# Which queue loads the weights of a scan's columns: SyncE's or GpSimd's

## The chip, the cores and the metric

The kernel runs on one core of one Trainium2 chip. The metric is the device time of one execution in microseconds. The engines are called as in the profile: PE (TensorE's matmuls), PEld (its weight loads), DVE (VectorE), ACT (ScalarE), POOL (GpSimd) and SP (SyncE, which here only issues DMAs). A DMA can be issued by SP or by POOL; each issues in the order of its own program, and a DMA that has to wait keeps all that stands behind it on that engine waiting.

## The reference

A trunk of two layers is applied to two groups of 512 tokens (s = 0 and 1) with 1024 channels, with the same weights. The first layer is a time mixing with a scan in both directions:

```
xn = rms_norm(x); lerp(j) = xn + (0.5*(x_prev + x_next) - xn) * mu[j]
r, k, v, z = lerp(0) @ w_r, lerp(1) @ w_k, lerp(2) @ w_v, xn @ w_z
for d in (forward, backward):
    decay, a = f(lerp(3+d)), g(lerp(5+d))          # two low-rank products each
    S_t = S_{t-1} (diag(decay_t) + a_t b_t^T) + v_t k_t^T ;  y_t = S_t r_t
x1 = x + rms_norm((norm(y_fwd + y_bwd) + bonus) * silu(z) @ w_o)
```

The second layer is attention in a neighbourhood of an 8 x 64 grid, with a gate:

```
q, k, v, z = split(rms_norm(x1) @ w_in + b_in)
out = x1 + rms_norm((attention(q, k, v, rpb) * silu(z)) @ w_ao + b_o)
```

All is float32.

## The kernel before

**Products with weights.** A weight matrix is cut into columns of 128 outputs. One column is a tile of 128 x 1024 (512 KB), loaded in two halves of 128 x 512 (256 KB) into the tile `raw`, which has three buffers (NRAW). Each half is split into a high and a low part (`whi`, a cast on ACT; `wlo`, a subtraction on DVE), and PE does three matmuls for each of the eight blocks of 128 inputs. Such a block of three matmuls is called a product below. A `raw` buffer is free again when the subtraction has read it. `whi` and `wlo` have four buffers each.

**Stages.** The prelude (to about 155 us) normalizes, makes the inputs and computes the first columns of s = 0. Then comes the scan (`scan_phase`, 155 to 1155 us): 8 blocks (two groups of tokens, four blocks of heads), each with 8 steps, one after the other. A step is a short chain through PE, ACT and DVE (`step`, `factors`, `near`, `outer`), and each block needs a preparation (`prep`: the decays, the tile `ab`, stored as `dab`) and an inverse of triangular matrices (`inverse`: the tile `MT`). Between these, PE computes 80 columns of weights, which are 160 halves: r and v of s = 0, k, r, v and z of s = 1, w_o, and 24 columns of w_in. The rest (`rest`, attention and the last products) follows to the end. It loads its weights with `self.load`, on SP.

**The columns in the scan** are `flow`. Its parts are generators: `loads` (line 719 issues a load), `splits` (line 726 the cast on ACT, line 728 the subtraction on DVE), `operands` (lines 752 and 754 split the inputs), `products` (lines 807 to 809) and `posts` (what is done with a column's result).

**The order.** A planner (`Clock` and `weave`) sets the order of PE, DVE and ACT in the scan. It keeps a rough time for each engine and lets that generator go on which can go on first. A DMA of SP's counts 380 ns of issue time in it, one of POOL's 900. Where nothing is ready for PE for some time, it puts in a fill matmul of 128x256 (line 1631), whose result nobody reads. The order of SP and POOL is then made by the framework's scheduler.

**Who issues what in the scan.** SP issues the weight loads, the loads of each step (`cab` from `dab`, `V` and `X` from `dvt`), those of each preparation (`k`, `r`, `rb`, `tmp` from the low-rank weights), the stores of `dab`, and the loads of the columns' inputs (`xr`). POOL issues the stores of the columns' results (`dr`, `dv`, `dk`, `dz`, `dq`, line 327; `dvt`, line 690) and of `dks`, and it fills small tiles: a column of `e` at each preparation (line 898) and half of `MT` at each inverse (line 1019, a pair of fills). Before the first block it fills the two `MT` tiles (line 1662). What goes to which queue is set here:

```
    def store(self, kind):
        return self.nc.gpsimd if self.away and kind not in ("y", "x1", "h") else self.nc.sync

    def load(self, dst, src):
        self.nc.sync.dma_start(dst, src)
        return dst
```

`away` is true in the scan alone.

Of the kernel before, what the change touches and what calls it, by code (L numbers as in the profile page):

```python
# [19 lines left out]
P = 128  # L20
# [211 lines left out]
class Trunk:  # L232
# [470 lines left out]
    def flow(self):  # L703


        nc, did, ck = self.nc, self.did, self.clock
# [3 lines left out]
        raw, w, x, todo = {}, {}, {}, {}  # L710
# [4 lines left out]
        def loads():  # L715
            for c, (_, _, src, _) in enumerate(cols):
                for j in range(2):
                    yield "S", lambda: did["load"] < did["split"] + self.NRAW
                    raw[2 * c + j] = self.load(self.t("raw", (P, self.WP), self.NRAW), src[:, j * self.WP:(j + 1) * self.WP])
                    did["load"] += 1  # L720

        def splits():
# [92 lines left out]
        def posts(a):  # L815
# [5 lines left out]
        few = lambda: did["split"] - did["k"] // 4 <= self.STOCK  # L821
        return [
            Thread(lambda: 0, loads()), Thread(lambda: 3 if few() else 9, splits()), Thread(lambda: 0, fetched()), Thread(lambda: 2.5, operands()),
            Thread(lambda: 0.6, residual()), Thread(lambda: 0.6, scaled()), Thread(lambda: 0.6, squares()),
            Thread(lambda: 9, products()), Thread(lambda: 2, posts(0)), Thread(lambda: 2, posts(1))]
# [1097 lines left out]
```

## Time and profile before

| | |
|---|---|
| time, median of 3 runs | 1673.4 us (1672.16 to 1676.07) |
| the profiled execution | 1673.62 us, span 1671.8 us |
| granted TensorE clock, mean | 0.974 |
| busy: PE, DVE, ACT, POOL | 1566.5, 1229.4, 982.8, 116.9 us |
| SP's hardware queue | 194144 packets, 301.84 MB |
| POOL's software queue | 10112 packets, 31.47 MB |

Shares and sums of the whole span mix the stages. The change lies in the scan, so its part is read by stretches. A row "A L1 <- B L2: t, n, m" in the view of waits says that engine A stood idle t us in all, n times, at most m us, ahead of an instruction of line 1, and that line 2 on engine B ended the wait. SPq is SP's queue of DMA issues.

### The profile page before, as it was taken

How to read it: one execution, taken by the hardware profiler on the slowest of the kernel's cores; microseconds unless marked ns; L12 is line 12 of the kernel's file. 1: busy time of each engine (PE TensorE's matmuls, PEld its weight loads, DVE VectorE, ACT ScalarE, POOL GpSimd, SP SyncE). 2: the span in 40 equal slices, each digit the busy share in tenths (PEclk: the TensorE clock that was granted, in tenths of full speed). 3: DMA queues.
4: the chain of work that ended last, by engine and by line, in shares of the span. 5: the costliest groups of instructions: out<-in, count | busy, mean ns of one | idle time of the engine just before them, and what ended most of it. 6: DMA issues, size and time to landing. Idle time of an engine off the chain costs nothing.

```text
span 1671.8 us, 46461 instructions
## 1 busy us (share of the span) xinstructions
PE 1566.5 (94%) x18834; PEld 1200.3 (72%) x18834; DVE 1229.4 (74%) x2725; ACT 982.8 (59%) x1977; POOL 116.9 (7%) x246
## 2 busy tenths in 40 slices
PE   7989897999999988999998999999999898999998
PEld 6867666776767766766776777777778687777776
DVE  8985667788877885897888897855676856554564
ACT  5443665766766667655675665454577655554562
POOL 0000102310101122000000000000000000000000
PEclk9989998999999997999998999999999999999999
DMA  6435678677687786776776665563774337545553
GB/s 210 164 126 187 200 259 270 199 240 225 214 258 239 220 268 184 232 249 198 239 235 217 204 225 189 169 193 128 269 239 150 116 114 263 178 158 176 160 175 107
DMA packets 204470, 336.27 MB, mean 201 GB/s; under 512 B 20928, under 2 KB 86592, under 8 KB 204256
## 3 DMA queue, kind: packets, MB, share of 16 engines
q1 hardware_dynamic: 194144, 301.84, 56.4%
q0 software_dynamic: 10112, 31.47, 5.7%
q8 instruction: 148, 2.42, 0.6%
q14 instruction: 66, 0.54, 0.1%
HBM read 227.71 MB, written 105.51 MB: 199 GB/s over the span
## 4 chain that ended last, share of the span: by engine, by line
PE 68%; DVE 12%; DMA 9%; ACT 7%; issue 4%; SPq 1%; DVEq 0%; ACTq 0%
PE pm L807 7%; PE pm L808 5%; PE pm L809 5%; PE pg L428 5%; PE pg L429 5%; PE pg L430 5%; PE pf L1095 3%; PE zy L1167 2%; PE us L1214 2%; PE sc L1442 2%; PE us L1194 2%; PE zy L1218 2%; PE po L1475 2%; PE pt L1460 2%; DMA dab<-ab 1%
## 5 line engine op out<-in xcount | busy, mean ns | idle before, releaser
L807 PE MATMUL pm<-act,whi 128*128 128x512 f32 x640 | 285.5, 446 | 12.7 <-ACT act L776 4.1
L808 PE MATMUL pm<-act,whi 128*128 128x512 f32 x640 | 256.5, 401 | 9.8 <-DVE act L754 5.9
L809 PE MATMUL pm<-act,wlo 128*128 128x512 f32 x640 | 255.7, 400 | 7.9 <-DVE wlo L728 7.8
L428 PE MATMUL pg<-act,whi 128*128 128x512 f32 x448 | 182.6, 409 | 6.1 <-ACT act L377 5.7
L429 PE MATMUL pg<-act,whi 128*128 128x512 f32 x448 | 178.0, 397 | 0.1
L430 PE MATMUL pg<-act,wlo 128*128 128x512 f32 x448 | 177.0, 395 | 0.0
L377 ACT CAST whi<-raw 128x512 fp32r<-128x512 f32 x148 | 91.5, 619 | 125.2 <-PE pg L429 80.7
L807 PEld LDWEIGHTS pm<-act,whi 128*128 128x128 f32 x640 | 122.0, 191 | 56.2 <-issue 11.6
L809 PEld LDWEIGHTS pm<-act,wlo 128*128 128x128 f32 x640 | 122.3, 191 | 38.9 <-DVE wlo L728 12.1
L378 DVE TENSOR_TENSOR wlo<-raw,whi 128x512 fp32r<-128x512 f32 x148 | 101.3, 687 | 66.0 <-ACT whi L377 58.8
L808 PEld LDWEIGHTS pm<-act,whi 128*128 128x128 f32 x640 | 122.8, 192 | 35.8 <-DVE act L754 11.1
L728 DVE TENSOR_TENSOR wlo<-raw,whi 128x512 fp32r<-128x512 f32 x160 | 108.9, 685 | 41.4 <-ACT whi L726 41.2
L726 ACT CAST whi<-raw 128x512 fp32r<-128x512 f32 x160 | 97.9, 618 | 55.4 <-PE pm L808 38.5
L428 PEld LDWEIGHTS pg<-act,whi 128*128 128x128 f32 x448 | 84.6, 189 | 24.8 <-ACT act L377 6.0
L430 PEld LDWEIGHTS pg<-act,wlo 128*128 128x128 f32 x448 | 84.8, 189 | 18.7 <-issue 1.2
L429 PEld LDWEIGHTS pg<-act,whi 128*128 128x128 f32 x448 | 84.9, 190 | 17.2 <-issue 1.7
L999 DVE TENSOR_TENSOR etmp<-N 128x30 f32<-128x30 f32 (+14 forms) x240 | 78.5, 327 | 4.1
L1001 DVE TENSOR_TENSOR N<-etmp,N 128x30 f32<-128x30 f32 (+14 forms) x240 | 78.5, 327 | 3.8
L1453 DVE CUSTOM_DVE_ANT_0 sb<-sc,bias 128x256 f32<-128x256 f32 x128 | 49.4, 419 | 28.9 <-PE pt L1460 22.9
L1456 ACT ACTIVATE sb<-sb,mx 128x256 f32<-128x256 f32 x128 | 64.0, 505 | 8.7 <-DVE mx L1455 8.6
L1206 ACT COPY X<-us 64x256 f32<-64x256 f32 x128 | 46.8, 366 | 35.6 <-PE zy L1073 32.9
L1095 PE MATMUL pf<-cab 64*64 64x128 f32 (+1 forms) x2048 | 66.3, 266 | 0.7 <-issue 0.7
(396 smaller groups left out, 3465.3 us busy)
## 6 DMA issues: line engine op xcount, KB each, us to landing
dab<-ab SPq DMA_DIRECT2D x32, 1024.0 KB
cab<-dab SPq DMA_DIRECT2D x64, 512.0 KB
raw<-in_w_in_dram SPq DMA_DIRECT2D x128, 256.0 KB
bias<-in_rpb_dram SPq DMA_DIRECT2D x32, 384.0 KB
raw<-in_w_z_dram SPq DMA_DIRECT2D x32, 256.0 KB
raw<-in_w_k_dram SPq DMA_DIRECT2D x32, 256.0 KB
raw<-in_w_r_dram SPq DMA_DIRECT2D x32, 256.0 KB
k<-dk SPq DMA_DIRECT2D x32, 256.0 KB
```

Of the source, the lines that this page charges most:

```text
L377: self.nc.scalar.copy(hi, src)
L378: (eng or self.nc.vector).tensor_tensor(lo, src, hi.bitcast(F32), op=ALU.subtract)
L428: nc.tensor.matmul(ps, hi, x[k][0], start=(k == 0), stop=False)
L429: nc.tensor.matmul(ps, hi, x[k][1], start=False, stop=False)
L430: nc.tensor.matmul(ps, lo, x[k][0], start=False, stop=(k == KT - 1))
L726: nc.scalar.copy(hi, raw[h])
L728: nc.vector.tensor_tensor(lo, raw.pop(h), hi.bitcast(F32), op=ALU.subtract)
L807: nc.tensor.matmul(ps, hi[:, at], xh, start=(k == 0), stop=False)
L808: nc.tensor.matmul(ps, hi[:, at], xl, start=False, stop=False)
L809: nc.tensor.matmul(ps, lo[:, at], xh, start=False, stop=(k == KT - 1))
L999: vt.tensor_tensor(tv, N[:, q + 1:, q:q + 1].broadcast_to([P, n, q]), N[:, q:q + 1, :q].broadcast_to([P, n, q]), op=ALU.mult)
L1095: end = nc.tensor.matmul(st.f[half(a), h, 0, d, g] if st.last else st.f[half(a), h, :, d, g], ab[half(h), d, g, 2 * e[d] + 1 - a], rt if s ...
```

## The change

In `loads`, the weight halves are issued with `nc.gpsimd.dma_start` in place of `self.load`. That is all; lines below 719 get a number that is one higher.

```
--- before.py
+++ after.py
@@ -716,7 +716,8 @@
             for c, (_, _, src, _) in enumerate(cols):
                 for j in range(2):
                     yield "S", lambda: did["load"] < did["split"] + self.NRAW
-                    raw[2 * c + j] = self.load(self.t("raw", (P, self.WP), self.NRAW), src[:, j * self.WP:(j + 1) * self.WP])
+                    raw[2 * c + j] = self.t("raw", (P, self.WP), self.NRAW)
+                    nc.gpsimd.dma_start(raw[2 * c + j], src[:, j * self.WP:(j + 1) * self.WP])
                     did["load"] += 1
```

All 160 weight loads of the scan go from SP's program to POOL's. The planner sees them as DMAs of POOL's, so the order of PE, DVE and ACT in the scan changes too.

POOL, at the beginning of the scan, before. `lm` is a tile of the prelude, `MT`, `e` and `dr` are those named above.

```order
L562 MEMSET lm_1296 128x1
L563 MEMSET lm_1296 128x1
L1662 MEMSET MT_439_1696 128x2048
L1662 MEMSET MT_440_1697 128x2048
L898 MEMSET e_490_1868 128x8
L327 DMA dr_463_1780<-tmp_1778 128x512
L327 DMA dr_478_1826<-tmp_1824 128x512
L898 MEMSET e_513_1980 128x8
```

POOL at the same place in the new program:

```order
L562 MEMSET lm_1296 128x1
L563 MEMSET lm_1296 128x1
L720 DMA raw_1746<-in_w_r_dram 128x512
L720 DMA raw_1766<-in_w_r_dram 128x512
L1663 MEMSET MT_439_1696 128x2048
L1663 MEMSET MT_440_1697 128x2048
L899 MEMSET e_490_1866 128x8
L720 DMA raw_1804<-in_w_r_dram 128x512
L720 DMA raw_1837<-in_w_r_dram 128x512
L327 DMA dr_462_1777<-tmp_1775 128x512
L720 DMA raw_1864<-in_w_r_dram 128x512
```

The first four weight loads stand ahead of the `MT` fills (two of them just before these rows), the fifth (raw_1804) and sixth behind them.

POOL in the middle of the columns of w_in, at about 1005 to 1021 us, before:

```order
L327 DMA dq_2558_14038<-tmp_14031 128x512
L327 DMA dk_2571_14102<-tmp_14096 128x512
L1019 MEMSET MT_439_1696 32x32x32 x2
L327 DMA dv_2582_14187<-tmp_14170 128x512
L327 DMA dz_2607_14401<-tmp_14366 128x512
```

and in the new program:

```order
L327 DMA dq_2561_14054<-tmp_14047 128x512
L720 DMA raw_14123<-in_w_in_dram 128x512
L327 DMA dk_2568_14102<-tmp_14089 128x512
L720 DMA raw_14172<-in_w_in_dram 128x512
L720 DMA raw_14234<-in_w_in_dram 128x512
L1020 MEMSET MT_439_1696 32x32x32 x2
L720 DMA raw_14278<-in_w_in_dram 128x512
L327 DMA dv_2581_14187<-tmp_14178 128x512
L720 DMA raw_14325<-in_w_in_dram 128x512
```

Weight loads now stand between the stores and behind the pair of `MT` fills.

SP ahead of the first scan step, before:

```order
L333 DMA raw_2933<-in_w_v_dram 128x512
L333 DMA k_2995<-dk_302_1318 128x512
L333 DMA dab_632_2489<-ab_2758 128x8x256
L333 DMA V_2774<-dvt_646_2523 128x256
L333 DMA X_2780<-dvt_646_2523 64x2x128
```

and in the new program:

```order
L333 DMA X_2939<-dvt_645_2536 64x2x128
L333 DMA k_2975<-dk_302_1318 128x512
L333 DMA V_2771<-dvt_645_2536 128x256
L333 DMA X_2777<-dvt_645_2536 64x2x128
L333 DMA V_2774<-dvt_645_2536 128x256
```

The weight load ahead of `k` and `V` is gone, and the store of `dab` follows later.

PE after the first group of columns' products, before:

```order
L807 MATMUL pm_2156<-act_1683,whi_2183 128x512
L808 MATMUL pm_2156<-act_1682,whi_2183 128x512
L809 MATMUL pm_2156<-act_1683,wlo_2184 128x512
L1631 MATMUL zy_1710<-cc 128x256 x2
L807 MATMUL pm_2240<-act_1641,whi_2226 128x512
```

and in the new program:

```order
L808 MATMUL pm_2158<-act_1683,whi_2185 128x512
L809 MATMUL pm_2158<-act_1682,whi_2185 128x512
L810 MATMUL pm_2158<-act_1683,wlo_2186 128x512
L1632 MATMUL zy_1710<-cc 128x256 x6
L808 MATMUL pm_2247<-act_1641,whi_2230 128x512
```

Six fill matmuls stand where there were two. Over the whole scan there are 105 before and 112 in the new program.

## The prediction

> **What bounds the kernel now.** I read the table of stages first, then the chain that ended last, then the waits of SP's queue and the rows of the weight tile, and last the queues around two places. Columns of the first view: stretch, then busy microseconds and instructions of PE, PEld, DVE, ACT and POOL, granted clock, DMA share, GB/s.
>
> ```profile
> 155.00:345.00 190.00, 167.40 (x1679) 127.91 (x1678) 134.78 (x240) 119.69 (x233) 36.94 (x61) 0.95 0.76 241
> 345.00:535.00 190.00, 178.00 (x3244) 128.70 (x3243) 162.00 (x317) 128.57 (x255) 17.26 (x34) 0.99 0.72 230
> 535.00:745.00 210.00, 193.98 (x3588) 146.84 (x3587) 160.88 (x311) 136.03 (x272) 34.53 (x58) 0.94 0.75 230
> 745.00:945.00 200.00, 182.62 (x3064) 139.12 (x3062) 168.26 (x334) 126.02 (x237) 9.33 (x19) 0.96 0.68 219
> 945.00:1155.00 210.00, 207.11 (x3909) 157.95 (x3891) 154.29 (x305) 110.32 (x214) 15.90 (x28) 1.00 0.60 190
> ```
>
> The scan lies between 155 and 1155 us, and only there does the change act. PE is busy 929.1 of its 1000 us: idle 22.6, 12.0, 16.0, 17.4 and 2.9 us in the five stages, 70.9 in all. So PE is the bound, and nothing that only makes transfers earlier can win more than those 70.9 us. DVE is the next (780), POOL is nearly free (114).
>
> ```profile
> by line: PE pm L807 12.0%; PE pm L808 8.8%; PE pm L809 8.8%; issue 5.8%; PE pf L1095 4.9%; PE zy L1167 3.4%; PE us L1214 3.4%; PE us L1194 3.2%; PE zy L1218 2.9%; DMA dab<-ab 2.3%; DVE ab L921 2.3%; DVE wlo L728 2.1%; PE pf L956 1.6%; PE zy
> 183.65 5.34 DMA tmp<-in_lora_dram
> 190.69 1.28 ACT L881
> 244.69 8.94 DMA raw<-in_w_v_dram
> 279.74 8.00 DMA V<-dvt
> 717.56 5.68 DMA V<-dvt
> ```
>
> These are the scan's part of the chain, its shares, and single pieces of it (start, length, what). It is mostly the columns' matmuls (L807 to L809); one weight load (8.94 us) and loads of V stand in it, nearly all before 345 us.
>
> **The queues.** From the waits of SP's queue, the rows of the weight tile, of the casts and of POOL's stores (durations minimum/median/maximum in ns):
>
> ```profile
> SPq L333 <- DVE wlo L728: 145.8, 78, 13.5
> L333 SPq DMA_DIRECT2D raw<-in_w_in_dram x128: 327/333/1822, 862.3 to 1586.7; - x128
> L327 POOL DMA_DIRECT2D dv<-tmp x22: 539/558/575, 255.1 to 1161.2; - x22
> DMA to landing us min/median/max: 2.3/4.5/7.7
> L726 ACT CAST whi<-raw x160: 601/619/648, 156.7 to 1151.3; 128x512 fp32r<-128x512 f32 x160
> L728 DVE TENSOR_TENSOR wlo<-raw,whi x160: 653/685/698, 157.3 to 1155.2; 128x512 fp32r<-128x512 f32 x160
> ```
>
> SP stands 145.8 us in the scan, 78 times, at loads whose buffer is not yet free (a buffer is free when L728 has read it). All that SP issues behind stands too. The landing row is that of POOL's 256 KB stores.
>
> How much cover has a weight load? The 160 casts L726 spread over 156.7 to 1151.3, one in 6.25 us. With three buffers, cast h comes on average 3 x 6.25 = 18.8 us after cast h-3, and the buffer frees 0.6 + 0.7 us after that one began. A landing of 4.5 us leaves 18.8 - 1.3 - 4.5 = 13 us. So the mean load may be held 13 us for nothing; only where casts crowd does a hold cost.
>
> **Part by part.**
>
> *Issue time.* 160 loads leave SP (160 x 0.333 = 53 us) and go to POOL; a POOL store of the same size takes 0.54, so 160 x 0.54 = 86 us. POOL goes from 114 to 200 busy of 1000. Nobody waits for either: zero, covered by POOL's 886 idle microseconds. The load's time to land I take as unchanged: 4.5 for POOL's stores is between the extremes that I have.
>
> *SP no longer stands at weight loads, and these get a queue of their own.* The start of the first scan step shows what stood behind one:
>
> ```profile
> 277.93 0.34 SPq L333 DMA_DIRECT2D raw<-in_w_v_dram  x1
> 279.74 1.88 SPq L333 DMA_DIRECT2D V<-dvt  x1
> PE zy L1173 <- DMA V<-dvt: 6.4, 1, 6.4
> ```
>
> V was issued 1.8 us behind a weight load that waited for its buffer, and PE then waited 6.4 us for V, on the chain. At most that 1.8 is won here. The weight load of 244.69 took 8.94 us, in SP's line with others; in its own queue it might take POOL's median 4.5, which wins 4.4. Together 6.2 at most, and 0 if the transfers are only as fast as the 16 DMA engines, which move 241 GB/s in that stage. I take half: -3.1.
>
> A rule of the Trainium skill is against even this: its page "DMA: Bandwidth & Descriptors", section "Issuing engines are not separate DMA queues", says that DMAs of all issuing engines run on the same 16 DMA engines, so a second issuer saves only the sequencer's issue time. By it the 8.94 stays, the term is -1.8 and the sum below 1679.5. The trace before holds no weight load of POOL's, so no row decides it.
>
> *Loads held by what stands ahead of them on POOL, at the scan's start.* By the order, the fifth and sixth weight load now stand behind the two MT fills (L1662) and the e fill (L898). Rows of POOL, then ACT:
>
> ```profile
> 184.49 3.56 POOL L1662 MEMSET MT<- 128x2048 f32 x2 [30.25 <-DMA raw<-in_w_r_dram]
> 187.99 0.11 POOL L898 MEMSET e<- 128x8 f32 x1
> 180.26 0.33 SPq L333 DMA_DIRECT2D raw<-in_w_r_dram  x1
> 189.54 0.63 ACT L866 ACTIVATE km<-rb 128x512 f32<-128x512 f32 x1
> 190.07 0.60 ACT L726 CAST whi<-raw 128x512 fp32r<-128x512 f32 x1
> 190.69 1.28 ACT L881 ACT_TABLE_LOAD   x1
> ```
>
> The fifth load went out at 180.26; now it can't before 187.99 + 0.11 = 188.1. It lands 2.3 to 7.7 us later, most likely 4.5: at 192.6, where ACT wants it at 190.07. ACT stands 2.5 us (0.3 to 5.7), and right behind stands L881 of the first preparation, a piece of the chain. PE has nothing that would pay for it: +2.5.
>
> *Loads held elsewhere.* The same happens where casts crowd and an MT fill (L1019) stands between loads:
>
> ```profile
> 1016.89 1.97 POOL L1019 MEMSET MT<- 32x1024 f32 x2 [2.13 <-issue]
> 1017.88 0.62 ACT L726 CAST whi<-raw 128x512 fp32r<-128x512 f32 x1
> 1024.19 0.62 ACT L726 CAST whi<-raw 128x512 fp32r<-128x512 f32 x1
> ```
>
> Three casts lie within 6.3 us; 6.3 - 1.3 - 4.5 leaves 0.5 us of cover, and the pair of fills takes 1.97: late by 1.5. There are eight such pairs, one for each block of the scan; elsewhere casts are 6.25 us apart and the cover of 13 us swallows it. I take one: +1.5, between 0 and 8 x 1.97 = 15.8. That last end would need all eight to be crowded.
>
> *Stores held by loads* (the other way round): a load that waits for its buffer keeps the stores behind it on POOL, as it kept SP, up to 13.5 us. What waits for these: the readers of dr, dk, dv in later blocks, and the e fill, which POOL did at least one preparation ahead. Zero; without that lead each would cost up to the 13.5.
>
> *The plan itself.* The planner counts a DMA of POOL's dearer, and so the order of PE, DVE and ACT is another throughout the scan. The one count in which the plans tell of waiting differs: PE's fill matmuls (L1631), which it gets only when nothing else is ready, are 105 in the order before and 112 in the new one.
>
> ```profile
> L1631 PE MATMUL zy<-cc 128*128 128x256 f32 x210 | 55.0, 396 | 0.5 <-ACT y L1233 0.5
> ```
>
> The row counts two records for each: 55.0 / 105 = 0.52 us. Seven more are +3.7. By the second step of the scan there are 48 instead of 35, and 16 products (L807 to L809) fewer have been done; later the new order makes up for it. What else the new order does no row shows: I bound it by a third of the scan's idle PE time on either side of zero before that +3.7, 70.9 / 3 = 24, and take none of it.
>
> **The sum.** Against the profiled execution, 1673.62 (its span 1671.8; the median of the runs is 1673.4, so nothing need be added): 1673.6 - 3.1 + 2.5 + 1.5 + 3.7 = 1678.2 us, slower by 0.3%. A measurement of this kernel can tell about 0.2%, 3.3 us, from no change, so this is just to be seen.
>
> **The rivals.**
>
> *SP's freedom is what counts (faster).* The holds are covered, the plan's fills were idle time anyway, and the full 6.2 come: 1673.6 - 6.2 = 1667.4. For it speak the 145.8 us of SP's standing, the largest wait of its queue, and V on the chain twice. Against it: ACT waited for weights only 13.5 us in the scan, by the cast's rows:
>
> ```profile
>   DMA raw<-in_w_r_dram: 4.8, 3
>   DMA raw<-in_w_v_dram: 4.6, 1
>   DMA raw<-in_w_z_dram: 3.4, 2
> ```
>
> (and 0.7 for the other two weights). Chance 0.27.
>
> *POOL's line becomes the bound (slower by much).* In each of the eight blocks an MT fill holds a load, ACT stands at its cast, and what ACT stands for delays the next store on POOL. The point from which it decides is a cast interval under (1.3 + 4.5 + 2.0) / 3 = 2.6 us. Price: 15.8 in place of 1.5, so 1692.5. Against it the mean interval of 6.25. Chance 0.13.
>
> *DVE keeps POOL from issuing (slower).* If an issue had to wait until a running DVE operation ends, each load would come up to 0.69 us (L728) later, and in eight crowded places that is 5.5: 1683.7. Against it: POOL's 22 dv stores took 539 to 575 ns each, with DVE busy 780 of 1000 us. The Trainium skill, "SBUF — State Buffer", section "SBUF: two separate sides", tells of such a lock for descriptors that GpSimd writes while VectorE holds the port that they share. The trace so far does not agree. Chance 0.05.
>
> *Nothing is seen.* Every load comes in its cover, the fills replace idle time: 1673.6. For it the mean cover of 13 us. Chance 0.19.
>
> **How the numbers follow.** My forecast has 0.36, of which 0.04 lie within 0.2% of no change. Faster 0.27; same 0.19 + 0.04 = 0.23; slower 0.32 + 0.13 + 0.05 = 0.50. The range runs from 1664 (the faster rival less 3.3, what a measurement can't tell) to 1693 (POOL's line). The plan's open bound would reach further both ways, and that is the fifth that I leave out.
>
> **What would show it.** Right: the first L1662 pair still at about 184.5, the fifth weight load's issue behind it at 188, ACT's cast waiting some 2.5 us there; ACT L726 waiting for raw over 13.5 us in all; SP's wait for L728 gone from the scan; POOL busy near 200 us; L1631 at 224 records and PE's idle time in 155 to 345 us above 22.6. Wrong: if ACT's wait for raw falls, or SP's other loads land earlier and the first V comes before 279.7, the faster rival holds. If ACT waits for raw 25 us or more, behind L1019 in most blocks, POOL's line holds. If POOL's issues grow beyond 0.6 us, DVE holds them. If none of these rows moves and the time does, the new order on PE decides, and my term for the plan is wrong.

## The result and the profile after

| | median | runs |
|---|---|---|
| before | 1674.61 us | 9, 1667.99 to 1679.37 |
| after | 1685.49 us | 9, 1680.01 to 1696.43 |
| ratio | 1.0061 | 95% interval 1.0040 to 1.0083 |

Slower by 0.6%, 10 to 11 us. Executions of one kernel spread over 11 to 16 us, and the profiled execution of after, 1696.43 us (span 1694.3), is the longest of its nine. So rows of one execution show places, and medians decide what a change is worth.

From the page of after: busy times, and what the two queues moved. From the view of stages: the same five stretches as before, and their sum.

```profile
PE 1573.7 (93%) x18848; PEld 1205.2 (71%) x18848; DVE 1228.0 (72%) x2725; ACT 986.2 (58%) x1977; POOL 203.4 (12%) x406
q1 hardware_dynamic: 171104, 259.89, 47.4%
q0 software_dynamic: 22912, 73.42, 13.7%
...
155.00:345.00 190.00, 171.38 (x1968) 131.20 (x1967) 135.72 (x244) 120.34 (x237) 54.00 (x95) 0.98 0.76 244
345.00:535.00 190.00, 177.34 (x2934) 130.37 (x2934) 155.56 (x303) 130.06 (x255) 34.69 (x67) 0.99 0.72 227
535.00:745.00 210.00, 189.84 (x3570) 144.46 (x3569) 157.68 (x309) 128.00 (x255) 50.94 (x86) 0.94 0.73 227
745.00:945.00 200.00, 172.64 (x2923) 129.14 (x2921) 163.60 (x311) 123.81 (x236) 21.07 (x41) 0.93 0.65 213
945.00:1155.00 210.00, 204.37 (x3782) 155.92 (x3782) 159.17 (x324) 114.76 (x217) 37.00 (x68) 1.00 0.59 193
sum 1000.00, PE 915.57 PEld 691.09 DVE 771.73 ACT 616.97 POOL 197.71; mean PE 183.11 PEld 138.22 DVE 154.34 ACT 123.39 POOL 39.54
```

The loads did move: 73.42 - 31.47 = 42 MB are now on POOL's software queue, and POOL is busy 197.7 us in the scan. PE is idle 18.6, 12.7, 20.2, 27.4 and 5.6 us in the five stages, 84.4 in place of 70.9. The first stage gained 4 us; the third and fourth lost 4 and 10.

The rows of the casts, of the weight loads and of who stands at them (the fill matmuls come last; durations minimum/median/maximum in ns):

```profile
L727 ACT CAST whi<-raw x160: 602/620/720, 158.0 to 1170.8; 128x512 fp32r<-128x512 f32 x160
L720 POOL DMA_DIRECT2D raw<-in_w_in_dram x48: 536/536/543, 879.2 to 1155.4; - x48
...
DMA to landing us min/median/max: 2.8/4.7/8.7
...
POOL raw L720 <- DVE wlo L729: 163.9, 74, 8.5
...
SPq L333 <- PE zy L1219: 196.7, 58, 31.1
...
SPq L333 <- DVE wlo L729: 2.4, 4, 0.8
...
PE zy L1174 <- DMA V<-dvt: 2.5, 1, 2.5
...
L1632 PE MATMUL zy<-cc 128*128 128x256 f32 x224 | 61.5, 413 | 0.9 <-ACT Z L1180 0.9
```

SP's standing at weight buffers is gone (145.8 to 2.4 us), and POOL stands there now. SP now stands longer at other loads: 196.7 us at those that wait for PE's L1219, in before 106.7 us for the same line, L1218 there. An issue takes POOL 536 ns. The last cast comes at 1170.8 in place of 1151.3.

### The profile page after: what moved, and what is told of

It reads as the page before. It is cut to its first block, busy times and chain, and to the rows that moved or that the text cites. A ratio compares the mean times of both kernels' runs of the same rounds, so it can differ in the third digit from the quotient of the medians.

```text
span 1694.3 us, 46448 instructions
## 1 busy us (share of the span) xinstructions
PE 1573.7 (93%) x18848; PEld 1205.2 (71%) x18848; DVE 1228.0 (72%) x2725; ACT 986.2 (58%) x1977; POOL 203.4 (12%) x406
## 3 DMA queue, kind: packets, MB, share of 16 engines
q1 hardware_dynamic: 171104, 259.89, 47.4%
q0 software_dynamic: 22912, 73.42, 13.7%
## 4 chain that ended last, share of the span: by engine, by line
PE 65%; DVE 13%; DMA 8%; ACT 8%; issue 6%; SPq 1%; POOL 0%; DVEq 0%; ACTq 0%; POOLq 0%
PE pm L808 7%; PE pg L428 6%; PE pg L429 6%; PE pg L430 5%; PE pm L809 5%; PE pm L810 5%; PE pf L1096 3%; PE zy L1168 2%; PE sc L1443 2%; PE us L1215 2%; PE us L1195 2%; PE po L1476 2%; PE zy L428 2%; PE zy L429 1%; PE zy L430 1%
## 5 line engine op out<-in xcount | busy, mean ns | idle before, releaser
L1457 ACT ACTIVATE sb<-sb,mx 128x256 f32<-128x256 f32 x128 | 64.2, 505 | 12.3 <-DVE mx L1456 12.2
L1119 DVE TENSOR_TENSOR AK<-zy,cc 128x256 f32<-128x256 f32 x63 | 26.5, 421 | 53.2 <-PE zy L1074 52.5
```

## The experiments

The diff does two things: it moves 160 loads to another queue, and it makes the planner write another order for PE, DVE and ACT. The first pair takes these apart.

**Queue alone, order alone.** In `Clock.one`, a weight load is booked on the engine that it is not issued from. In the changed kernel:

```
         name = lambda x: x.bass_ap.tensor.name
+        if e == "G" and name(outs[0]).startswith("raw"):
+            e = "S"
```

Then POOL issues, and PE, DVE and ACT keep the order of before, but for three rows of DVE's and one of ACT's at the scan's start (165 to 180 us).

> GpSimd issues the weight loads as in the changed kernel, but the planner books them at SyncE's 380 ns, so that the order on PE, DVE and ACT is word for word that of the kernel before. Theory P (the new order on PE, DVE and ACT makes the difference): no slower than before, ratio 1.000 within 0.2%, or a little faster if SyncE's freedom still counts (down to -3 us). Theory Q (the loads come later from GpSimd's queue, held by its stores and fills): as slow as the changed kernel, ratio 1.006, +10 us.

Measured: 1.0076, interval 1.0049 to 1.0103.

In the kernel before, the other way round (`e == "S"` becomes `"G"`): SP issues, in the order of after.

> The other half: SyncE issues the weight loads as before, but the planner books them on GpSimd at 900 ns, so that the order on PE, DVE and ACT is that of the changed kernel. Theory P: as slow as the changed kernel, ratio 1.006 (+10 us), with the gap of about 20 us at the end of the scan (945 to 1180 us). Theory Q: as before, ratio 1.000 within 0.2%.

Measured: 1.0064 (1.0040 to 1.0089). Each half alone costs as much as both together; neither theory is right by itself, and the two costs don't add.

**Other orders.** If an order costs 11 us, is that the price of POOL's 900 ns or of any new order? The number at which a weight load is booked was changed, and nothing else:

```
-                self.t[e] = issued = max(issued, self.t["P"]) + 380.0
+                self.t[e] = issued = max(issued, self.t["P"]) + (333.0 if name(outs[0]).startswith('raw') else 380.0)
```

> The kernel before with one number of the planner changed: a weight load on SyncE is booked at 333 ns (its measured issue time) instead of 380. No queue changes; the order on PE, DVE and ACT is a new one. Theory P says that a new order by itself moves the time by some us either way: over 0.2% from 1.000 with a chance of two in three, bounds plus and minus 24 us. Theory Q: within 0.2% of before.

Measured: 1.0059 (1.0038 to 1.0079). The same on POOL's side, 540 in place of 900:

> The changed kernel with a weight load on GpSimd booked at 540 ns (its measured issue time) instead of 900. The loads' queue is that of the changed kernel; the order is a third one. Theory P: a time of its own, not tied to 1.006, anywhere within 24 us of before. Theory Q: 1.006 as the changed kernel, within 0.2%.

Measured: 1.0153 (1.0124 to 1.0182). To see the queue's part in these two orders, each was run with the other issuer, booked alike:

> The order that the planner makes with a load at 333 ns, with GpSimd issuing the loads. Its partner with SyncE issuing had 1.0059. Theory T (the order of before is one that its own queue fits unusually well, so that every change of order or of queue loses about 0.6%, and the queue by itself is worth nothing on average): 1.004 to 1.008, within 0.3% of its partner. Theory Q (the queue costs some 0.7% in every order): 1.013.

Measured: 1.0121 (1.0096 to 1.0147).

> The order that the planner makes with a load at 540 ns, with SyncE issuing the loads. Its partner with GpSimd issuing had 1.0153. Theory T: within 0.3% of its partner, 1.012 to 1.018. Theory Q (the queue costs some 0.7% in every order): 1.008.

Measured: 1.0076 (1.0049 to 1.0102). Theory Q named both values, T missed both: the queue has a price of its own. Two more orders with SP issuing:

> The kernel before with a weight load booked at 400 ns instead of 380: SyncE issues, and the order departs from that of before from the second block on. Theory T (the order of before is unusually good and nearly every other one is worse): 1.003 to 1.009. Theory N (orders scatter evenly about before): as likely under 1.000 as over it.

Measured: 1.0001 (0.9984 to 1.0018). This was hardly a new order: in the trace the instructions of PE, DVE and ACT follow one another as in before up to about 1000 us, but for two places of PE's. So it tells little between T and N.

> The same with 430 ns, a fifth order. Theory T: 1.003 to 1.009. Theory N: as likely under 1.000 as over it.

Measured: 1.0092 (1.0068 to 1.0116). All together, against before:

| a load is booked at | SP issues | POOL issues |
|---|---|---|
| 333 ns | 1.0059 | 1.0121 |
| 380 ns (order of before) | 1 | 1.0076 |
| 400 ns | 1.0001 | |
| 430 ns | 1.0092 | |
| 540 ns | 1.0076 | 1.0153 |
| 900 ns (order of after) | 1.0064 | 1.0061 |

By rows: POOL's queue costs 0.6 to 0.8% in three orders and nothing that can be told in the fourth, the one that after has. By the column of SP: the four orders that part from before's well ahead of the scan's end (three near its start, that of 430 ns at about 740 us) are all slower, by 0.6 to 0.9%, whether the load was booked cheaper or dearer; the fifth, nearly the same one, equals it. So, as far as four orders tell, it is not POOL's 900 ns that costs, but leaving the order of before.

**Where the queue's price arises.** Queue alone (POOL issues) and before have the same instructions in the same order (but for the four rows), so each one's start can be subtracted: ACT's lag is 4.0 us at 260, 9.8 at 289, 11.7 at 345, 9.6 at 800 and 14.7 at the scan's end. This compares one execution with one; they are 19.9 us apart, the medians 13.7. The step at 289, from the chain of queue alone (start, length, what), its timeline and its stages:

```profile
281.24 2.84 DMA dvt<-vs
284.12 13.45 DMA V<-dvt
297.69 0.71 PE zy L1176 x16
...
283.31 0.70 SPq L335 DMA_DIRECT2D dab<-ab  x1
284.12 0.59 SPq L335 DMA_DIRECT2D V<-dvt  x1
284.76 2.24 SPq L335 DMA_DIRECT2D X<-dvt  x1
287.11 1.87 SPq L335 DMA_DIRECT2D V<-dvt  x1
...
282.25 0.57 POOL L722 DMA_DIRECT2D raw<-in_w_v_dram  x1 [0.31 <-DVE wlo L731]
287.24 0.57 POOL L722 DMA_DIRECT2D raw<-in_w_v_dram  x1
...
PE zy L1176 <- DMA V<-dvt: 12.2, 1, 12.2
...
285.00:290.00 5.00, 0.53 (x20) 0.29 (x12) 4.86 (x11) 0.57 (x1) 2.51 (x4) 1.00 1.01 307
290.00:295.00 5.00, 0.00 (x0) 0.00 (x0) 0.00 (x0) 0.00 (x0) 0.00 (x0) 0.50 0.97 276
```

And SP's timeline of before, at the same instructions:

```profile
278.54 0.33 SPq L333 DMA_DIRECT2D k<-dk  x1
279.26 0.38 SPq L333 DMA_DIRECT2D dab<-ab  x1
...
281.67 2.07 SPq L333 DMA_DIRECT2D X<-dvt  x1
283.84 1.59 SPq L333 DMA_DIRECT2D V<-dvt  x1
285.48 1.39 SPq L333 DMA_DIRECT2D X<-dvt  x1
286.96 0.79 SPq L333 DMA_DIRECT2D raw<-in_w_v_dram  x1
```

The last weight load of these rows is the same one in both. In before its buffer is free at 282.7, and until 286.96 it stands on SP's line behind the V and X loads that PE waits for. From POOL it goes out 0.4 us after its buffer is free, 3.1 us after the first V (287.24 against 284.12; before 7.2 us after, 286.96 against 279.74), and runs beside V and the 1 MB `dab` store ahead of it. V's issue is 4.4 us later than in before, about the lag that was there at 260; what is new is the landing: `dab` landed 12.8 us after its issue (before 7.7), V 13.4 (8.0). From 290 to 295 every engine stands still, and the DMA engines are 97% busy. So V came late here by its transfer, not by its issue.

It is so beyond this place. Counted in the traces, SP's transfers issued from 155 to 1155 us (weight loads left out) that landed over 8 us after their issue; one has landed at the last count on its semaphore before that semaphore is used again:

| order | SP issues the loads | POOL issues them |
|---|---|---|
| 333 | 20 of 559 | 38 of 554 |
| 380 | 8 of 559 | 26 of 561 |
| 540 | 8 of 558 | 29 of 554 |
| 900 | 16 of 560 | 49 of 558 |

They are `dab`, `cab`, V, X, `xr` and `r` for the most part. Transfer by transfer the mean grows by 0.2 to 0.3 us. The count is no measure of the price: it grows most in the order of 900, where POOL's queue costs nothing that can be told. The weights themselves come a little later too. In queue alone ACT stood 18.4 us for weights at the scan's casts (in before 13.5), and a load landed 4.8 us after its issue in the median (4.4):

```profile
  ACT whi L729: 18.4, 10
DMA to landing us min/median/max: 2.8/4.8/9.7
```

**By blocks.** POOL issues the first 40 loads or the other 120, in the order of before:

```
-                    nc.gpsimd.dma_start(raw[2 * c + j], src[:, j * self.WP:(j + 1) * self.WP])
+                    q = nc.gpsimd if 2 * c + j < 40 else nc.sync
+                    q.dma_start(raw[2 * c + j], src[:, j * self.WP:(j + 1) * self.WP])
```

> The order of before on PE, DVE and ACT; GpSimd issues only the first 40 of the scan's 160 weight loads (to about 385 us), SyncE the other 120. Theory L (the cost of GpSimd's queue under the old order arises at a few places, 11.7 of its lag by 345 us, where a 1 MB store and the V load behind it on SyncE's queue landed after 12.8 and 13.4 us instead of 7.7 and 8.0 because GpSimd's transfers ran beside them): +8 to +11 us, ratio 1.005 to 1.006. Theory U (the cost accrues evenly over the loads): 40 / 160 of 13 us, so +3, ratio 1.002.

Measured: 1.0047 (1.0027 to 1.0067).

> The complement: SyncE issues the first 40 loads, GpSimd the other 120, old order. Theory L: +3 to +4 us, ratio 1.002. Theory U: 120 / 160 of 13, so +10 us, ratio 1.006. If the free queue is worth something behind the first block, it comes out below 1.000.

Measured: 1.0028 (1.0014 to 1.0043). Together 0.75%, which is the 0.76 of all 160; a load among the first 40 costs some five times one of the others (0.47 / 40 against 0.28 / 120). Theory L is the nearer. Its one place doesn't repeat in every execution, though: in the profiled one of the first 40, PE waited 7.5 us for that V, not 12.2.

**Bytes or queue?** Contention and late issue both belong to a load of POOL's. A load of an eighth keeps the issue, the holds, the buffers and the waits, and takes the bytes away:

```
-                    nc.gpsimd.dma_start(raw[2 * c + j], src[:, j * self.WP:(j + 1) * self.WP])
+                    nc.gpsimd.dma_start(raw[2 * c + j][:, :self.WP // 8], src[:, j * self.WP:j * self.WP + self.WP // 8])
...
+                part = raw.pop(h)[:, :self.WP // 8].unsqueeze(1).broadcast_to([P, 8, self.WP // 8])
+                cut = lambda x: x.rearrange("p (a b) -> p a b", a=8)
-                nc.scalar.copy(hi, raw[h])
+                nc.scalar.copy(cut(hi), part)
...
```

The subtraction reads `part` in the same way. The planner books it as a whole load, so the order is that of before but for at most some 20 rows an engine, at the scan's start and behind its end.

> The old order with GpSimd issuing the scan's weight loads, but each load brings only an eighth of its columns (32 in place of 256 KB, same number of loads, issues, buffers and waits; the cast and the subtraction read that eighth eight times over, so that their size stays; the weights are therefore not the reference's). To be read against its partner with SyncE issuing. Theory S (the queue costs because the loads' bytes run beside SyncE's transfers, which land later): GpSimd's version at most 0.2% above SyncE's, 3 us. Theory H (the loads themselves come later from GpSimd: longer issue, holds behind stores and fills): still 0.7% above it, +10 to +13 us.

Measured: 0.9949 (0.9930 to 0.9968).

> The partner: SyncE issues the loads of an eighth. Both theories: no slower than before, 0.990 to 1.000 of it, since 36 MB fewer are moved. Theory S: GpSimd's version within 0.2% of this one. Theory H: this one 0.7% below GpSimd's.

Measured: 0.9951 (0.9932 to 0.9969). The difference of 0.76% is gone. Rows of the eighth from POOL: its issue and its standing, and PE's wait for V; then that wait with SP issuing:

```profile
L724 POOL DMA_DIRECT2D raw<-in_w_in_dram x48: 534/534/542, 860.6 to 1129.7; - x48
...
  POOL raw L724: 192.7, 80
...
PE zy L1180 <- DMA V<-dvt: 6.7, 1, 6.7
```

```profile
PE zy L1180 <- DMA V<-dvt: 6.4, 1, 6.4
```

POOL issues as long (534 ns) and stands as long (192.7 us) as with whole loads (198.6), and it costs nothing. The late landings are gone with the bytes: 5 of SP's transfers landed over 8 us after their issue with POOL issuing the loads, 6 with SP. So H falls as far as issue and holds go, and the price lies in what the loads move. Two things are not told apart. An eighth lands sooner itself (3.5 us in the median from POOL, a whole load 4.8), and ACT stood 9.8 us for weights in place of 18.4; how much of the price is SP's late transfers, and how much the weights' own later landing, no run shows. And from POOL the packets of a load fall with its bytes (80 to 32; from SP they stay 144), by the queues' totals.

No version beat the kernel before with the whole weights.

## Why the prediction was right, and where its sum was not

The direction was right and the time lay in the range, but the rise of 10 to 11 us is a little over twice the forecast 4.8 (1678.2 less 1673.4), and it was in good part luck that it came out so. Of the sum's four terms only the plan's had a real cost behind it, and that one was 10.7 us, not 3.7; the two holds cost nothing, and the gain did not show.

- *SP's standing, -3.1.* This step failed, first in its reading. V was not kept by the weight load ahead of it. It waits for the store of `dvt` that POOL issued at 276.49 and that landed 2.9 us later, at 279.4, and the `dab` store ahead of it on SP waited until 279.56 for DVE. So of the 1.8 us at most 0.3 could be won. Rows of before (POOL's timeline, the chain), then the chain in the order of after, with POOL and with SP issuing the weights (there 276.16 is the issue of a weight load):

```profile
276.49 1.40 POOL L690 DMA_DIRECT2D dvt<-vs  x2 [0.37 <-issue]
279.23 0.33 DVE N L1001
279.56 0.07 SPq L333
279.74 8.00 DMA V<-dvt
...
276.63 5.28 DMA V<-dvt
...
276.16 0.34 SPq L335
276.62 5.33 DMA V<-dvt
```

  In the order of after V goes out at the same time in both, in the second with a weight load right ahead of it; PE waited 2.5 us for it with POOL issuing and 3.4 with SP, in before 6.4. It was the order that brought V forward. The load of 8.94 us took 6.5 in queue alone and 7.3 in after (9.1 with SP issuing in after's order), not 4.5. And the bounds left a loss out: with the order of before kept, the queue alone cost 0.76%, some 13 us. What I had read as SP's trouble, weight loads and step loads in one line, was also what kept weights behind the step's loads. In the order of after the queue is worth nothing that can be told, 1.0061 with POOL and 1.0064 with SP, to within some 0.3% (5 us) either way.
- *The plan, +3.7 and an open bound of 24.* That a new order costs was right, the size was not, and the fills that I sized it by did not show it. The seven more are there (224 records, 61.5 us in place of 55.0), but the order alone cost 0.64%, 10.7 us, within the bound of which I took nothing. The fills grew most in the first stage, where PE's idle time fell; with SP issuing in after's order the idle time arises later, 23.9 and 6.9 us from 745 on against 17.4 and 2.9 before:

```profile
745.00:945.00 200.00, 176.07 (x3114) 132.37 (x3112) 169.28 (x329) 127.59 (x244) 8.35 (x18) 0.96 0.68 218
945.00:1155.00 210.00, 203.10 (x3768) 154.53 (x3767) 153.97 (x309) 110.89 (x211) 15.35 (x27) 0.99 0.60 190
```

- *The fifth load, +2.5.* The hold came as forecast and cost nothing, by the timeline of after:

```profile
182.84 3.55 POOL L1663 MEMSET MT<- 128x2048 f32 x2 [21.85 <-DVE mrx L1653]
186.33 0.11 POOL L899 MEMSET e<- 128x8 f32 x1
186.38 1.06 POOL L720 DMA_DIRECT2D raw<-in_w_r_dram  x2
191.96 0.61 ACT L727 CAST whi<-raw 128x512 fp32r<-128x512 f32 x1
```

  It landed at 190.8, 4.4 us after its issue, and in the new order ACT wanted it at 192.0. I had set the load's new time against the cast's old one.
- *Loads held elsewhere, +1.5.* Seven later loads of after were held 1.2 to 3.2 us on POOL, and each had landed before its cast's turn came, so none cost ACT anything. From the free buffer to the issue it takes 0.3 us in the median, at most 0.6 in nine of ten.
- *Issue time and stores held by loads, 0.* Right: 536 ns, and POOL's stores and fills in queue alone go out at most 1.8 us later than the work around them.
- *The rivals.* POOL's issue of a weight load took 0.58 us at most, but for the first one's 0.68, so DVE doesn't keep it. POOL's line didn't become the bound. SP's freedom is not seen by itself in any row of the table. Of the signs that I named, ACT's wait for weights and V's issue pointed at the faster rival (in after ACT waited 8.8 us, not 13.5), and the time rose. V's issue came from the order, as shown above, so that sign could not tell a queue's effect from an order's. PE's idle time from 155 to 345 us, which was to rise, fell to 18.6. The last of the signs, that the new order on PE decides and the plan's term is wrong, is what the pair above bears out.

The Trainium skill, "DMA: Bandwidth & Descriptors", section "Issuing engines are not separate DMA queues", was weighed in the prediction: a second issuer saves the sequencer's issue time alone. The runs agree that it brings no more bandwidth: in the first stage 228 GB/s were moved in queue alone and 241 in before. They go further, since in three orders of four the saved issue time came with a loss. For that the same page, section "Queues, rings and completion order", has a rule that I did not use: each DMA engine takes turns between the queues that have work for it, packet by packet. The stretch above shows both queues at work at once: from 283 to 297.6 us POOL's had 37.1% of the engines and SP's 51.9%, while SP's V stood on the chain. It shows no more than that, since in before, from 279 to 287.7, the shares were 38.0% and 62.6%; turns by packet no run here shows.

## What to carry to other kernels

A queue's order is also a priority: before moving bulk loads off a line on which urgent small loads stand, look at what runs beside those then, where the DMA engines are near full, and at what the small loads themselves wait for: here V waited for a store, and a free line could not bring it forward. Where a planner writes the order, separate the two effects by booking a step as before while issuing it anew, and compare that with the order alone; a few neighbouring orders tell how much any new order moves the time. A hold on a load is priced against the consumer's time in the new order, not in the old one.

## What the runs showed that was not expected

- A load of 256 KB is 144 packets from SP (194144 - 171104 over 160) and 80 from POOL (22912 - 10112 over 160), an eighth of it 144 and 32. Its issue hardly depends on its size: in the rows of w_in 333 ns from SP and 536 from POOL for whole loads, 338 and 534 for an eighth.
- 160 loads of an eighth, 36.7 MB less of 336, made the kernel 0.5% faster, with PE busy 929.8 of the scan's 1000 us from POOL, before 929.1: that much less to move changed PE's share in the scan by next to nothing.
- Open: why the order of after takes POOL's queue for nothing where three others pay 0.6 to 0.8% for it, and what makes the order of before better than the four new ones. Neither was settled by these runs. What the queue's price in the other three is made of, SP's late transfers or the weights' own later landing, is open too.
